# The first block of a two-layer kernel: the bias loaded and turned between the row tiles of x, the second half's turns elsewhere, nine of twelve products in 512 columns

## The chip, the cores and the metric

The kernel runs on one core of one Trainium2 chip. The metric is the device time of one execution in microseconds. Lower is better.

## The reference

```python
batch, m, k, h, n = 16, 512, 768, 3072, 768
y = np.matmul(x, w1) + b1          # x: 16 x 512 x 768, w1: 768 x 3072, b1: 3072
y = np.maximum(y, 0)
return np.matmul(y, w2)            # w2: 3072 x 768
```

All inputs and the output are float32. With the batch flattened x has 8192 rows.

## The kernel before

**Blocks.** The 8192 rows are cut into eight blocks of 1024 rows, and the 3072 hidden columns into two chunks of 1536. The kernel goes through the eight blocks with the first chunk, then through them again with the second: 16 rounds of a first phase (x times w1, bias, relu) and a second phase (the result y times w2). The weights of a chunk and one block of x lie in SBUF in float16. In most rounds both phases are done with fewer products than the plain scheme needs: sums and differences of tiles are formed first (VectorE; lines 828 for x, 844 for w1, 862 for w2, 1046 for y), the products of the sums are made on TensorE (line 1073 in the first phase, 1199 in the second), and their results are combined by VectorE and ScalarE (lines 1109 to 1124 and 1210 to 1216). A combination may also put a start value into the PSUM bank of a chain of products that follows, a "seed"; operation 16 of the first phase (line 1124) is one.

**The first block** (`first_block`, with the first chunk) is different. Its data have only just been loaded, so its first phase uses plain products. x arrives as row tiles of 128 rows and has to be turned (transposed) 128 x 128 at a time. The 1024 rows are eight row tiles: 0 to 3 are the first half (m = 0), 4 to 7 the second (m = 1). Tiles 0 to 3 come in float32 on the queues of SyncE and ScalarE (line 711), are turned by TensorE (line 925) into PSUM, and copied to `x` as float16, one part of each tile by VectorE (line 933) and one by ScalarE (line 931). Tiles 4 to 7 come through GpSimd's queue as float16 into `xn` (line 706) and are turned in the same way. w1 comes in six strips of 256 columns (line 685), w2 in twelve pieces (line 691), on GpSimd's queue too.

A product of the first block (`add_plain`, matmuls in line 983) is named by strip, by j (128 of the strip's 256 columns) and by the half m; it goes over 768 rows of w1 in six steps and has 512 columns of x. With `parts=2` it is made in two halves of 256 columns, 12 matmuls, of which the first half reads only the first two row tiles of its half of x; with `parts=1` in six matmuls of 512 columns, which need all four tiles. ScalarE applies bias and relu and writes y (line 992), for `evict_parts=2` in two pieces. Before the change the twelve products of the strips 0 to 2 all have `parts=2`; the twelve of the strips 3 to 5 have `parts=1`.

**The bias.** `load_bias` (line 679) loads it as 24 rows of 128 on ScalarE's queue. `add_bias` turns it on TensorE (line 945), copies it from PSUM (line 948, VectorE) and forms twelve small operations for the tables of the later rounds (lines 959 and 963) and one for a check (line 951), all on VectorE.

**What sets the order.** Every piece of work is a task of a planner (`Graph`): engine, expected length, what it reads and writes. TensorE's tasks run in the order in which they are added. For VectorE, ScalarE, GpSimd and SyncE the planner simulates the run and picks, among the tasks that can start, the one that is due first; some tasks are only fitted into gaps. It also picks the PSUM bank of each product or turn, among those that come free. `presets` gives it the times at which the first loads land, among them that of the bias (`b1_rows`). The instructions are then written in the planned order, and each engine runs its own in that order.

Of the kernel before, what the change touches and what calls it, by code (L numbers as in the profile page):

```python
# [586 lines left out]
class Fast:  # L587
# [120 lines left out]
    def prologue(self):  # L708
        nc = self.nc
        for s in range(4):  # L710
            (nc.sync, nc.scalar)[s % 2].dma_start(out=self.s[:, s],
                                                  in_=self.xf[s * P:(s + 1) * P, :])
        self.load_bias()
        self.load_strip(self.v1, 0, 0, 0)
        self.constants()
        self.load_strip(self.v1, 0, 0, 1)
        self.load_strip(self.v1, 0, 0, 2)
        self.load_x(0, 1, 2)
        for h in range(3):
            self.load_strip(self.v1, 0, 1, h)  # L720
        for q in range(4):
            for h in range(3):
                self.load_w2(self.v2, 0, h, q)
        self.load_x(1, 0)
        for _ in range(8):
            nc.tensor.matmul(self.ps[:, 7, 0:P], lhsT=self.ones, rhs=self.ones, start=True,
                             stop=True)

    def presets(self):
        g = self.g  # L730
        for t, at in enumerate((9.3, 11.3, 13.3, 19.9, 21.8, 23.8)):
            for k in range(2):
                g.preset(("w1", t // 3, 2 * (t % 3) + k), at)
        for q in range(4):
            for h in range(3):
                for n in range(2):
                    g.preset(("w2", 2 * q + n, h), 24.8 + 3 * q + h)
        for s in range(4):
            g.preset(("xn", 4 + s), 15.2 if s < 2 else 17.2)
            g.preset(("xn", s), 39.5)  # L740
            g.preset(("rows", s), (5.3, 5.3, 7.2, 7.2)[s])
        g.preset("b1_rows", 5.0)

# [264 lines left out]
    def first_block(self):  # L1010
        for s in range(4):
            self.add_transpose_first(0, s)
        plain = self.add_plain
        for strip in range(3):
            for j in range(2):
                between = None
                if strip == 0 and j == 0:
                    between = self.add_bias
                elif strip == 2 and j == 1:
                    between = lambda: [self.add_transpose_first(1, s) for s in (0, 1)]  # L1020
                plain(strip, j, 0, 2, 2 if strip == 1 else 1, between)
        plain(0, 0, 1, 2, 1, lambda: [self.add_transpose_first(1, s) for s in (2, 3)])
        plain(0, 1, 1, 2, 1)
        for strip in (1, 2):
            for j in range(2):
                plain(strip, j, 1, 2, 2 if strip == 1 else 1)
        for strip in (3, 4, 5):
            for m in range(2):
                for j in range(2):
                    plain(strip, j, m, 1, 1)  # L1030
# [514 lines left out]
```

## Time and profile before

| | |
|---|---|
| Device time, median of 3 runs | 849.0 us (848.92 to 849.01) |
| Span of the profiled execution | 847.4 us |
| TensorE busy | 839.4 us, 99% |
| VectorE busy | 737.9 us, 87% |
| ScalarE busy | 569.4 us, 67% |
| First product of the first block starts | 9.46 us |
| Second phase of the first block starts | 42.96 us |
| First phase of the second block starts | 68.31 us |

The profile is of one execution, and shows for every engine when each instruction ran and what ended the idle time ahead of it. Its span goes from the first instruction to the end of the last and is 1.6 us shorter than the median device time, which also counts what lies around it. PE is TensorE, PEld its weight load, DVE is VectorE, ACT ScalarE, POOL GpSimd and SP SyncE. In timelines a row is the start, the length, the engine, line and operation, what it writes and reads, how many neighbours of one kind are merged (x12), and in brackets the idle time ahead of it with what ended it. Times in the text are counted from the start of the span. Matmuls are pipelined and their recorded lengths overlap, so their rate is read from starts.

### The profile page before, as it was taken

The page shows a single profiled execution, that of the slowest core. Times are in us where ns is not written, and L with a number is a line of the kernel's source. Part 1 is how long each engine was busy: PE and PEld are TensorE (multiplying, and loading weights), DVE is VectorE, ACT ScalarE, POOL GpSimd, SP SyncE. Part 2 cuts the span into 40 slices and gives each one's busy share as a digit, 9 for nine tenths or more (in the row PEclk, how much of TensorE's full clock was granted, in tenths as well). Part 3 has the DMA queues.
Part 4 walks back from the last instruction along what each step waited for, and adds up shares of the span by engine and source line. Part 5 has one row for each costly group of instructions (what it writes and reads, how often), then busy time and mean ns, then how long its engine had stood idle before and what let it go on. Part 6 is the DMA issues. An engine that isn't in the chain of part 4 may idle for free. (4 is left out here: it accounts for less than half of the span.)

```text
span 847.4 us, 16784 instructions
## 1 busy us (share of the span) xinstructions
PE 839.4 (99%) x6381; PEld 625.5 (74%) x6381; DVE 737.9 (87%) x1231; ACT 569.4 (67%) x1203; POOL 164.1 (19%) x179
## 2 busy tenths in 40 slices
PE   8999999999999999999999999999999999999997
PEld 7558778686786867768687686877868678686874
DVE  5898987969889697998999979798896979979788
ACT  5866876778677695756858558766757666456463
POOL 5210011102111010010030503224041230501300
PEclk9999999999999999999999999999999999999999
DMA  9996497978988678594793977979789797985836
GB/s 213 202 180 176 81 233 105 163 183 133 222 113 148 169 126 192 95 223 150 224 187 65 192 123 124 187 106 178 125 128 150 116 173 113 147 134 75 146 117 169
DMA packets 170967, 128.93 MB, mean 152 GB/s; under 512 B 93804, under 2 KB 169348, under 8 KB 170884
## 3 DMA queue, kind: packets, MB, share of 16 engines
q0 software_dynamic: 56560, 68.82, 53.1%
q1 hardware_dynamic: 113856, 58.02, 28.3%
q8 instruction: 50, 0.82, 0.4%
q10 hardware_dynamic: 468, 1.00, 0.3%
q14 instruction: 33, 0.27, 0.1%
HBM read 73.54 MB, written 69.21 MB: 168 GB/s over the span
## 5 line engine op out<-in xcount | busy, mean ns | idle before, releaser
L1199 PE MATMUL ps<-v,y 128*128 128x384 f16 x2496 | 408.4, 326 | 0.0
L1073 PE MATMUL ps<-x,v 128*128 128x256 f16 x3600 | 395.7, 273 | 0.0
L1073 PEld LDWEIGHTS <-v 128*128 128x128 f16 x3600 | 352.2, 98 | 42.4 <-issue 0.2
L1199 PEld LDWEIGHTS <-y 128*128 128x128 f16 x2496 | 244.2, 98 | 160.0 <-issue 0.2
L1210 ACT ACTIVATE s<-ps 128x384 f32<-128x384 f32 (+1 forms) x244 | 153.0, 646 | 121.3 <-PE ps L1199 120.2
L1046 DVE TENSOR_TENSOR y<-y 128x768 f16<-128x768 f16 (+1 forms) x384 | 219.4, 619 | 2.6
L1116 DVE CUSTOM_DVE_ANT_0 y<-ps,s 128x512 f16<-128x512 f32 x240 | 156.0, 686 | 54.4 <-ACT s L1113 41.4
L1252 POOL DMA_DIRECT2D out_dram<-s x78 | 93.9, 1470 | 145.4 <-ACT s L1210 97.0
L1113 ACT ACTIVATE s<-ps,bt 128x256 f32<-128x256 f32 x180 | 75.3, 470 | 62.5 <-PE ps L1073 56.7
L828 DVE TENSOR_TENSOR x<-x 128x768 f16<-128x768 f16 (+1 forms) x210 | 113.7, 579 | 1.3
L1113 ACT ACTIVATE y<-ps,bt 128x256 f16<-128x256 f32 x180 | 69.5, 486 | 10.8 <-PE ps L1073 10.8
L1210 ACT ACTIVATE ps<-ps 128x384 f32<-128x384 f32 (+1 forms) x144 | 67.9, 509 | 8.1 <-PE ps L1199 6.6
L1216 DVE TENSOR_TENSOR s<-ps,s 128x768 f32<-128x768 f32 x74 | 70.5, 953 | 1.2 <-issue 0.3
L706 POOL DMA_DIRECT2D xn<-in_x_dram x30 | 25.9, 863 | 214.0 <-DMA x<-xn 99.5
L1216 DVE TENSOR_TENSOR s<-s,ps 128x768 f32<-128x768 f32 x60 | 57.1, 951 | 2.2 <-DVE s L1216 0.5
L767 ACT ACTIVATE junk<-xn 128x768 f16<-128x768 f16 x64 | 54.0, 843 | 0.3
L1255 POOL DMA_DIRECT2D out_dram<-s x15 | 17.7, 1181 | 169.5 <-ACT s L1210 157.7
L1113 ACT ACTIVATE ps<-ps,bt 128x256 f32<-128x256 f32 x60 | 26.7, 445 | 32.4 <-PE ps L1073 31.4
L1109 ACT ACTIVATE ps<-ps 128x512 f32<-128x512 f32 x60 | 35.3, 588 | 4.1 <-DVE y L1116 3.5
L1124 DVE TENSOR_TENSOR s<-s,ps 128x512 f32<-128x512 f32 x30 | 20.6, 688 | 17.7 <-PE ps L1073 17.7
L983 PE MATMUL ps<-x,v 128*128 128x256 f16 (+1 forms) x216 | 32.0, 308 | 0.7 <-DVE x L933 0.7
L1119 DVE SCALAR_TENSOR_TENSOR s<-ps,bt,s 128x256 f32<-128x256 f32 x60 | 26.1, 477 | 4.4 <-PE ps L1073 4.4
(60 smaller groups left out, 304.8 us busy)
## 6 DMA issues: line engine op xcount, KB each, us to landing
out_dram<-s POOLq DMA_DIRECT2D x93, 384.0 KB, 8.8
out_dram<-s SPq DMA_DIRECT2D x70, 384.0 KB, 6.6
xn<-in_x_dram POOLq DMA_DIRECT2D x28, 768.0 KB, 9.7
x<-out_dram SPq DMA_DIRECT2D x7, 384.0 KB, 3.5
v<-in_w_dram POOLq DMA_DIRECT2D x6, 384.0 KB, 10.6
v<-in_w_dram POOLq DMA_DIRECT2D x12, 192.0 KB, 9.1
w1d<-in_w_dram POOLq DMA_DIRECT2D x6, 384.0 KB, 6.5
w2d<-in_w_dram POOLq DMA_DIRECT2D x12, 192.0 KB, 4.9
```

The lines of the kernel that those rows point to most:

```text
L767: self.nc.scalar.activation(out=self.junk, in_=self.xn[:, s, :], func=ACTF.Square, accum_out=self.stat[:, self.stat_at["x"] + i:][:, 0:1])
L828: self.nc.vector.tensor_tensor(out=self.two(x, out), in0=self.two(x, in0), in1=self.two(x, in1), op=ALU.add if sign > 0 else ALU.subtract)
L983: nc.tensor.matmul(self.ps[:, ps.at[0], cols], lhsT=self.v1[:, gi, 2 * h + k2, k, j * P:(j + 1) * P], rhs=rhs, start=(k2 == 0 and k == 0), ...
L1046: self.nc.vector.tensor_tensor(out=self.two(self.y, out), in0=self.two(self.y, in0), in1=self.two(self.y, in1), op=ALU.add if sign > 0 els ...
L1073: nc.tensor.matmul(self.ps[:, at, j * self.QM:(j + 1) * self.QM], lhsT=self.v1[:, gi, self.w1s[c][gi][FIRST_V[p]], k, j * P:(j + 1) * P], ...
L1109: nc.scalar.activation(out=out, in_=ps, scale=float(a), func=func if kind == "out" else ACTF.Copy)
L1113: nc.scalar.activation(out=out[:, j], in_=ps[:, j], func=func, scale=float(a), bias=beta(j))
L1116: nc.vector._custom_dve(TENSOR_ADD_SAT, out=out, in0=ps, in1=s, s0=F_MAX, s1=0.0)
L1199: nc.tensor.matmul(self.ps[:, bank[ch].at[j], 0:NH], lhsT=self.y[:, ys[SECOND_U[p]], m0:m0 + P], rhs=self.v2[:, slot[SECOND_V[p]], h, :], ...
L1210: nc.scalar.activation(out=out, in_=ps, func=ACTF.Copy, scale=float(a))
L1216: engine.tensor_tensor(out=out, in0=in0, in1=in1, op=ALU.add if a == b else ALU.subtract)
L1252: nc.gpsimd.dma_start(out=rows, in_=out, accum_op=ALU.add)
```

## The change

It has four parts, all in the first block.

- The bias is loaded on ScalarE's queue between its two row tiles (1 and 3), and no longer behind both. The planner is told that it lands at 6.0 us instead of 5.0.
- The bias is turned after the row tiles 0 and 1 and ahead of 2 and 3, and no longer between the two halves of the first product.
- The turns of tiles 4 and 5 stand ahead of the product of strip 2, j = 1, and no longer between its halves. The turns of tiles 6 and 7 stay behind the first half of the first product of m = 1, but the whole product of j = 1 now comes behind them, ahead of that product's second half.
- Nine of the twelve products have `parts=1`. Two halves are kept for strip 0 with j = 0 and m = 0, and for strip 0 with m = 1 (both j). Every eviction is one piece.

```diff
@@ prologue
         for s in range(4):
             (nc.sync, nc.scalar)[s % 2].dma_start(out=self.s[:, s],
                                                   in_=self.xf[s * P:(s + 1) * P, :])
-        self.load_bias()
+            if s == 1:
+                self.load_bias()
@@ presets
-        g.preset("b1_rows", 5.0)
+        g.preset("b1_rows", 6.0)
@@ first_block
         for s in range(4):
             self.add_transpose_first(0, s)
+            if s == 1:
+                self.add_bias()
         plain = self.add_plain
+
+        def turns(*tiles):
+            for s in tiles:
+                self.add_transpose_first(1, s)
         for strip in range(3):
             for j in range(2):
-                between = None
-                if strip == 0 and j == 0:
-                    between = self.add_bias
-                elif strip == 2 and j == 1:
-                    between = lambda: [self.add_transpose_first(1, s) for s in (0, 1)]
-                plain(strip, j, 0, 2, 2 if strip == 1 else 1, between)
-        plain(0, 0, 1, 2, 1, lambda: [self.add_transpose_first(1, s) for s in (2, 3)])
-        plain(0, 1, 1, 2, 1)
+                if strip == 2 and j == 1:
+                    turns(0, 1)
+                plain(strip, j, 0, 2 if strip == 0 and j == 0 else 1, 1)
+        plain(0, 0, 1, 2, 1, lambda: [turns(2, 3), plain(0, 1, 1, 2, 1)])
         for strip in (1, 2):
             for j in range(2):
-                plain(strip, j, 1, 2, 2 if strip == 1 else 1)
+                plain(strip, j, 1, 1, 1)
```

## The prediction

> **What bounds the kernel now.** I read the page's head first, then the waits of TensorE, then TensorE's instructions in order of time, and last VectorE in the stretches where TensorE never waits.
>
> ```profile
> span 847.4 us, 16784 instructions
> PE 839.4 (99%) x6381; PEld 625.5 (74%) x6381; DVE 737.9 (87%) x1231; ACT 569.4 (67%) x1203; POOL 164.1 (19%) x179
> ```
>
> TensorE (PE) is busy for 839.4 of 847.4 us. The view of waits, for TensorE alone, says where the rest is:
>
> ```profile
> PE ps L726 <- DVE ones L666: 1.3, 1, 1.3
> PE ps L925 <- DMA s<-in_x_dram: 1.1, 2, 0.6
> PE ps L983 <- DVE x L933: 0.7, 2, 0.3
> ```
>
> Every wait belongs to the first block; L1073 and L1199, the lines of all later products, have none. So a microsecond won or lost in the first block reaches the end whole, as long as the other engines can follow. The timeline of TensorE (start, length, what, and the idle time ahead of it) shows the block:
>
> ```profile
> 5.55 1.50 PE L925 MATMUL ps<-ident,s 128*128 128x128 f32 x12 [0.48 <-DMA s<-in_x_dram]
> 7.64 1.50 PE L925 MATMUL ps<-ident,s 128*128 128x128 f32 x12 [0.58 <-DMA s<-in_x_dram]
> 9.46 0.82 PE L983 MATMUL ps<-x,v 128*128 128x256 f16 x6 [0.32 <-DVE x L933]
> 10.21 0.24 PE L945 MATMUL ps<-ident,b_rows 24*128 24x24 f32 x1
> 10.38 6.72 PE L983 MATMUL ps<-x,v 128*128 128x256 f16 x60
> 16.93 0.83 PE L925 MATMUL ps<-ident,xn 128*128 128x128 f16 x12
> 17.61 1.59 PE L983 MATMUL ps<-x,v 128*128 128x256 f16 x12
> 19.03 0.83 PE L925 MATMUL ps<-ident,xn 128*128 128x128 f16 x12
> 20.21 22.91 PE L983 MATMUL ps<-x,v 128*128 128x256 f16 x138 [0.35 <-DVE x L933]
> ...
> 42.96 25.51 PE L1199 MATMUL ps<-v,y 128*128 128x384 f16 x156
> 68.31 26.36 PE L1073 MATMUL ps<-x,v 128*128 128x256 f16 x240
> ```
>
> The lengths overlap by a pipeline's depth, so I go by starts. 60 matmuls of 256 columns run from 10.38 to 16.93: 0.1092 us each, 0.655 for six, which is half a product.
>
> **The change part by part.** The instruction order of the changed kernel, which can be built, differs on VectorE (DVE) only in its first 117 planned tasks, on ScalarE (ACT) in about its first 70, and on GpSimd and SyncE nowhere. From about 80 us on it is the same program. The question is therefore how many microseconds earlier TensorE comes out at 80 us.
>
> *Bias turn taken out of the first product.* Six matmuls start at 9.46 and the next six at 10.38: 0.92, where six take 0.655. The bias costs 0.265 there, and this goes. In its new place, after the first two tiles, TensorE ends at 5.55 + 1.50 = 7.05 and waits for row tile 2 until 7.64; the bias's 0.24 fits into that hole, if the bias has landed. For its landing:
>
> ```profile
> DMA to landing us min/median/max: 4.3/5.1/6.1
> ```
>
> This is the row tiles' line (L711): from issue to landing 4.3 us for the first, 6.1 for the last, so they land from 5.3 to 7.5. The bias now stands between ScalarE's two tiles. I take a landing before 7.05, at no cost, and keep 7.5 as the upper end. Row tile 3 is issued 0.65 us later, but needs to be there only when its turn comes, near 8.4 (the middle of the group of turns at 7.64), and the tile ahead of it in its queue lands only at 5.3. I cost it at nothing; landing after 8.4 it would cost one for one.
>
> *The bias tables now stand ahead of the tiles' copies.* This is the term that speaks against the change. VectorE's timeline of before:
>
> ```profile
> 6.11 1.21 DVE L933 CAST x<-ps 128x384 f16<-128x384 f32 x2 [4.87 <-PE ps L925]
> 8.19 1.21 DVE L933 CAST x<-ps 128x384 f16<-128x384 f32 x2 [0.87 <-PE ps L925]
> 10.48 0.18 DVE L948 COPY b1y<-ps 128x24 f32<-128x24 f32 x1 [1.07 <-PE ps L945]
> 10.70 0.24 DVE L959 TENSOR_SCALAR bt<-b1y 128x8 f32<-128x8 f32 x2
> 10.98 0.17 DVE L963 TENSOR_TENSOR bt<-bt,b1y 128x8 f32<-128x8 f32 x1
> 11.06 0.31 DVE L959 TENSOR_SCALAR bt<-b1y 128x8 f32<-128x8 f32 x3
> 11.41 0.17 DVE L963 TENSOR_TENSOR bt<-bt,b1y 128x8 f32<-128x8 f32 x1
> 11.49 0.17 DVE L959 TENSOR_SCALAR bt<-b1y 128x8 f32<-128x8 f32 x1
> 11.69 0.37 DVE L963 TENSOR_TENSOR bt<-bt,b1y 128x8 f32<-128x8 f32 x2
> ```
>
> In the changed order the copy of the bias and seven table operations stand between the copies of tile 1 and tile 2, and two more between tile 2 and tile 3. Eight such operations take 11.49 - 10.48 = 1.01; they start when tile 1's copy ends, at 7.32, so tile 2's copy starts at 8.33 instead of 8.19. It takes 0.6; two table operations, the second waiting for the first, take 0.20 + 0.08; so tile 3's copy starts near 9.2 and ends at 9.75, where it ended at 8.19 + 1.21 = 9.40. Neighbours that do not wait for each other overlap by up to 0.08, so the delay lies between about 0.15 and 0.35. Does TensorE wait for it? The first product reads only tiles 0 and 1, yet before it waited for "DVE x L933" until 9.46: it uses the PSUM bank that tile 3's copy leaves, and by the changed plan it still does. So the first product starts **0.25 later**. The first strip of w1 hides nothing of it; TensorE's weight load waited for it until 9.32 only:
>
> ```profile
> 9.32 0.67 PEld L983 LDWEIGHTS <-v 128*128 128x128 f16 x6 [0.42 <-DMA v<-in_w_dram]
> ```
>
> The Trainium skill, "VectorE: DVE Perf Modes", section "The DRAIN you can't avoid", says that the next operation does not start until the pipe is empty, and that a semaphore between two costs nothing extra. By that the ten operations would take their full lengths and the first product would start about 0.7 later. The row with three operations in 0.31 us speaks against it; it is a rival below.
>
> *The second half's turns.* The first pair (tiles 4 and 5) stood between two halves of a product and costs 17.61 - 16.93 = 0.68; so it does in its new place. The second pair takes 20.21 - 19.03 = 1.18, so **0.50** of it is a wait for the copies. Now half a product (0.655) that needs only tiles 4 and 5 comes behind it, more than the 0.50: the wait goes, with 0.15 to spare. The twelve matmuls at 17.61 take 19.03 - 17.61 = 1.42 instead of 1.31, a further **0.11** behind ScalarE's copy of tile 5, which ends at 17.47 + 0.86 = 18.33; a whole product of 1.3 us now covers it. That row, and those of the loads of x (L706):
>
> ```profile
> 17.47 0.86 ACT L931 COPY x<-ps 128x384 f16<-128x384 f16 x2 [0.30 <-PE ps L925]
> ```
>
> ```profile
> L706 POOL DMA_DIRECT2D xn<-in_x_dram x2: 718/726/735, 5.6 to 6.3; - x2
> ...
> DMA to landing us min/median/max: 9.5/10.1/10.8
> ```
>
> Tiles 4 and 5 land at 5.6 + 9.5 = 15.1, tiles 6 and 7 at 6.3 + 10.8 = 17.1. The new turns start near 9.71 + 1.31 + 4 x 1.30 = 16.2 and 18.8. Both in time.
>
> *Nine products in 512 columns.*
>
> ```profile
> L983 PE MATMUL ps<-x,v 128*128 128x512 f16 x72 | 15.7, 379 | 0.0
> ```
>
> From 20.21 to 42.96 run 66 matmuls of 256 and these 72 of 512: (22.75 - 66 x 0.1092) / 72 = 0.216 each. A product takes 1.296 instead of 1.310; nine save **0.13**. ScalarE's evictions in one piece save it time too, but it is no bound there.
>
> Shift of TensorE when the block ends: -0.265 - 0.50 - 0.11 - 0.13 + 0.25 = **-0.76 us**.
>
> *What is late next.* VectorE. It starts the sums of the last strips when the strip lands, at 23.72, and the strip does not land sooner because TensorE is early. From there it has hardly a gap:
>
> ```profile
> 23.72 1.15 DVE L844 TENSOR_TENSOR v<-v 128x768 f16<-128x768 f16 x2 [1.36 <-DMA v<-in_w_dram]
> ```
>
> ```profile
> 43.00:60.00 17.00, 16.93 (x28) 1.00 0.92 171
> 60.00:76.40 16.40, 15.98 (x27) 1.00 0.94 246
> 76.40:80.60 4.20, 2.16 (x5) 1.00 0.00 0
> ```
>
> (stretch, its length, VectorE's busy time.) Until 76.4 it is full; only then does it catch up. The changed order puts sums that nobody needs yet behind those that TensorE waits for, which covers TensorE's lead to about 75 us. But by operation 16 of the next block (L1124, the seed of chain 0) the same work is behind it in either order:
>
> ```profile
> 76.42 0.70 DVE L1124 TENSOR_TENSOR ps<-s,ps 128x512 f32<-128x512 f32 x1 [0.21 <-issue]
> ```
>
> It can start about 0.2 earlier, not 0.76: it ends between 76.7 and 76.9. The fifteenth product of the block reads it. It started at 68.31 + 14 x 0.655 = 77.48 and would now start at 76.72. I take **0.15 lost** there (bounds 0 and 0.3). After that VectorE idles, and the rest moves as one.
>
> Sum: -0.76 + 0.15 = -0.6 us: a span of 846.8. The span is 1.6 below the median of the runs; with the same around it, 849.0 becomes **848.4**.
>
> **The rivals.**
>
> 1. *Nothing lost on VectorE*: the table operations overlap fully, tile 3's copy is hidden and operation 16 is in time. -0.265 - 0.50 - 0.11 - 0.13 = -1.0: 848.0. For it: 0.21 us of VectorE's time before L1124 was idle. Against it: the first product waited for just this copy.
> 2. *VectorE takes it all back.* Between 43 and 76.4 it has 0.07 + 0.42 = 0.5 us of idle time to cover a lead of 0.76; if the new order makes one more gap, the lead is gone by 80 us: 848.9 to 849.0.
> 3. *Pipe drains between the small operations*: eight in 8 x 0.17 = 1.36 and two more in 0.34, tile 3's copy ends at 10.1, the first product starts 0.7 later; -1.0 + 0.7 = -0.3: 848.7. For it: those that wait for their neighbour are 0.20 apart. Against it: three in 0.31. It is the rule of the Trainium skill named above.
> 4. *The bias lands late, the other side.* TensorE runs in order, so the bias turn holds tiles 2 and 3, and VectorE's ten operations start 0.3 after it. Before, its landing was covered until 10.21. The moment that decides is about 7.7 us: then the first product starts 1.0 later than before and nothing is won; each microsecond beyond costs one. At 8.5 it is 849.8. Against it: the third issue of ScalarE, as the bias then was, already moved its data by 6.95:
>
> ```profile
> q10 hardware_dynamic: 50, 0.02, 9.4%
> ```
>
> (ScalarE's queue from 6.20 to 6.95 us: 50 packets of 0.4 KB on average, where a row of x has 3 KB and one of the bias 0.5 KB: this is the bias.) In front of tile 3 it can hardly be later.
>
> 5. *It does not do what it says*: the wait of 0.50 comes back at the second half of the product behind the turns, where tiles 6 and 7 are read. Then -0.6 + 0.5: 848.9.
>
> **How the numbers follow.** Forecast (848.1 to 848.7) 0.64; rival 1 0.10; rival 2 0.10; rival 3 0.06; rival 4 0.05; rival 5 0.05. The range: rival 1, with the 0.14 by which the first product could start before 9.46, gives 847.85; rival 2 with a stall of 0.15 more gives 849.15. So 847.8 to 849.2; outside it lies rival 4 and little else. 0.2% (1.7 us, about what a measurement of this kernel can tell from no change) is more than every term here together: to be faster by that, the block would have to lose more waiting than the 1.0 it has; to be slower, the bias would have to land after 9.4 us. Chances: faster 0.03, within 0.93, slower 0.04.
>
> **What would show it.** In the changed kernel's profile: the bias matmul near 7.0, inside the idle time ahead of 7.64; tile 3's copy on VectorE ending at 9.6 to 9.75, and the first product 0.05 behind it; two groups of turns near 16.2 and 18.8 without the 0.35 of idle time; L1199 first at 42.2; a short wait of TensorE at L1073 near 76.8 for "DVE ps L1124"; L1199 again at 93.9, 0.6 before the 68.31 + 240 x 0.1092 = 94.5 of now. A bias matmul after 7.7, a wait behind the second turns, or waits for VectorE between 43 and 75 us would prove me wrong.

## The result, and the profile after

The changed kernel takes **850.39 us** (median of 19 runs, 849.91 to 851.95); beside it on the same chip the kernel before takes 848.88 (19 runs, 848.82 to 849.15). The ratio is 1.0021, interval 1.0015 to 1.0028: 1.5 us slower, where 0.6 us faster was forecast (849.0 to 848.4), and above the forecast's range (847.8 to 849.2). The changed kernel's times also spread over 2 us, those of before over 0.3.

The profiled execution took 851.14 us, its span is 849.5, 2.1 more than before. I read it in the order of the forecast: TensorE's waits, its first instructions, then VectorE; and last the end of the kernel, which the forecast had not looked at. TensorE's waits in the changed kernel:

```profile
PE ps L984 <- DVE x L934: 1.8, 1, 1.8
PE ps L727 <- DVE ones L666: 1.3, 1, 1.3
PE ps L926 <- DMA s<-in_x_dram: 0.5, 1, 0.5
```

The three waits for DMA and VectorE of before have become one of 1.8 us. TensorE's timeline:

```profile
5.57 1.95 PE L926 MATMUL ps<-ident,s 128*128 128x128 f32 x12 [0.50 <-DMA s<-in_x_dram]
7.45 0.24 PE L946 MATMUL ps<-ident,b_rows 24*128 24x24 f32 x1
...
10.95 6.65 PE L984 MATMUL ps<-x,v 128*128 128x256 f16 x36 [1.79 <-DVE x L934]
17.44 0.83 PE L926 MATMUL ps<-ident,xn 128*128 128x128 f16 x12
18.11 2.11 PE L984 MATMUL ps<-x,v 128*128 128x512 f16 x12
20.06 0.83 PE L926 MATMUL ps<-ident,xn 128*128 128x128 f16 x12
20.73 22.85 PE L984 MATMUL ps<-x,v 128*128 128x256 f16 x114
43.41 25.51 PE L1202 MATMUL ps<-v,y 128*128 128x384 f16 x156
```

The first product starts at 10.95 instead of 9.46, 1.49 later. From there to the second phase it is 32.46 us instead of 33.50: 1.04 less, close to the 0.265 + 0.50 + 0.11 + 0.13 = 1.005 of the forecast. So the second phase starts 0.45 late.

Part of the 1.49 is TensorE's clock. The twelve turns at 5.57 take 1.95 instead of 1.50. In the trace the record of the granted clock begins, at 1.0, at 6.50 us in this run and at 5.54 in the profile of before; the turns start 0.21 to 0.24 apart ahead of that moment and 0.11 apart behind it. VectorE shows the rest:

```profile
7.23 0.56 DVE L934 CAST x<-ps 128x384 f16<-128x384 f32 x1 [0.19 <-PE ps L926]
7.72 0.18 DVE L949 COPY b1y<-ps 128x24 f32<-128x24 f32 x1
7.94 0.70 DVE L960 TENSOR_SCALAR bt<-b1y 128x8 f32<-128x8 f32 x2
8.68 0.17 DVE L964 TENSOR_TENSOR bt<-bt,b1y 128x8 f32<-128x8 f32 x1
8.76 0.71 DVE L960 TENSOR_SCALAR bt<-b1y 128x8 f32<-128x8 f32 x3
...
9.59 0.56 DVE L934 CAST x<-ps 128x384 f16<-128x384 f32 x1
```

Two table operations take 0.70 and three take 0.71, where before they took 0.24 and 0.31. One line's durations (least, median, most, in ns), of after:

```profile
L960 DVE TENSOR_SCALAR bt<-b1y x8: 163/169/629, 7.9 to 11.0; 128x8 f32<-128x8 f32 x8
```

and of before:

```profile
L959 DVE TENSOR_SCALAR bt<-b1y x8: 165/165/254, 10.7 to 12.1; 128x8 f32<-128x8 f32 x8
```

Most still take 0.17, but some take 0.63. What ran beside those? GpSimd, which writes the descriptors of the loads of w1:

```profile
6.96 2.50 POOL L685 DMA_DIRECT2D v<-in_w_dram  x3
9.98 0.70 POOL L691 DMA_DIRECT2D v<-in_w_dram  x1 [0.52 <-DMA v<-in_w_dram]
```

Three issues follow one another from 6.96 to 9.46. In the trace the second ends at 8.646 and the third at 9.463; the long operations of VectorE end at 8.643, 9.462 and 9.472. Not every one is held: the first, at 7.941, takes 0.172, although the second issue has run since 7.770. Before, GpSimd did the same from 6.98 to 9.47, but VectorE had its tables at 10.70.

Now the end. The branch behind the last product gives the point at which TensorE is through; after and before:

```profile
L1515 PEldq COMPARE_BRANCH  x2: 95/202/310, 841.9 to 843.2; - x2
...
L1515 PEldq EVENT_SEMAPHORE  x1: 51/51/51, 843.1 to 843.1; - x1
```

```profile
L1512 PEldq COMPARE_BRANCH  x2: 90/135/180, 841.3 to 842.6; - x2
...
L1512 PEldq EVENT_SEMAPHORE  x1: 51/51/51, 842.5 to 842.5; - x1
```

TensorE is through 0.6 later (843.1 against 842.5), but the span is 2.1 longer. **1.5 us are lost when TensorE has nothing left to do.** The view of the DMA from 840 to 850 us, in 40 slices of 0.25 us, of after:

```profile
GB/s 197 0 0 221 387 326 369 381 375 369 326 387 363 362 381 375 99 307 344 422 338 357 356 344 350 266 25 31 25 57 25 25 6 0 0 0 0 0 0 0
...
q8 instruction: 1, 0.02, 0.6%
...
out_dram<-s ACTq DMA_DIRECT2D x1, 192.0 KB, 4.3
out_dram<-s SPq DMA_DIRECT2D x1, 192.0 KB, 4.2
```

and of before:

```profile
GB/s 43 344 375 326 399 357 356 375 332 375 381 375 369 307 123 356 369 362 387 369 356 363 387 113 0 0 0 33 0 0 0 0 0 0 0 0 0 0 0 0
...
out_dram<-s ACTq DMA_DIRECT2D x1, 192.0 KB, 2.5
out_dram<-s SPq DMA_DIRECT2D x1, 192.0 KB, 2.6
```

Before, the stores run at about 370 GB/s and stop. After, they stop likewise, and then 25 GB/s go on for 1.5 us: about a sixteenth of the full rate, so one DMA engine of 16 works on alone. The last stores land after 4.2 instead of 2.6 us. What is new beside them is one packet of 16 KB in a queue of kind "instruction". In the trace it starts at 844.84 and takes 0.945 us; before, the last one of its kind runs at 837.4. Both kernels have 50 of these over the run. They follow TensorE's instructions (12,730 before, 12,620 after): from one packet to the next TensorE starts 255 matmuls and weight loads on average, so a packet holds about 256. In the trace the stores' packets keep 16.3 to 16.9 at a time busy where no such packet runs, and 15.2 to 15.9 from 844.4 to 845.8: about one engine of 16 is lost to them for 1.4 us. The packet is on record for 0.945 of that; what holds the engine ahead of it is not shown.

### The profile page after: what moved, and what is told of

The parts are those of the page before. It is cut to its first block, busy times and chain, and to the rows that moved or that the text cites. A ratio compares the mean times of both kernels' runs of the same rounds, so it can differ in the third digit from the quotient of the medians.

```text
span 849.5 us, 16673 instructions
## 1 busy us (share of the span) xinstructions
PE 839.4 (99%) x6327; PEld 620.6 (73%) x6327; DVE 738.6 (87%) x1231; ACT 568.5 (67%) x1199; POOL 164.0 (19%) x179
## 5 line engine op out<-in xcount | busy, mean ns | idle before, releaser
L1116 ACT ACTIVATE y<-ps,bt 128x256 f16<-128x256 f32 x180 | 69.5, 486 | 10.8 <-PE ps L1076 10.8
L984 PE MATMUL ps<-x,v 128*128 128x512 f16 (+1 forms) x162 | 31.6, 355 | 1.8 <-DVE x L934 1.8
## 6 DMA issues: line engine op xcount, KB each, us to landing
v<-in_w_dram POOLq DMA_DIRECT2D x6, 384.0 KB, 10.7
```

The source lines that it names most:

```text
L984: nc.tensor.matmul(self.ps[:, ps.at[0], cols], lhsT=self.v1[:, gi, 2 * h + k2, k, j * P:(j + 1) * P], rhs=rhs, start=(k2 == 0 and k == 0), ...
L1116: nc.scalar.activation(out=out[:, j], in_=ps[:, j], func=func, scale=float(a), bias=beta(j))
```

## The experiments

Two theories. **A**: the table operations with one input are held while GpSimd writes descriptors, and hold the copies of tiles 2 and 3 behind them; rival: so many small operations are simply long; second rival: TensorE's clock, which comes up at different times, makes tile 1 and all behind it late. **B**: with 110 instructions fewer on TensorE one more fetch of instructions falls among the last stores and delays them; rival: the late end follows from the late beginning. A third, **C**, came up on the way: a lead of TensorE is used up by 500 us in every plan. All numbers, with the difference to the kernel before on the same chip (us; "fetch" is a 16 KB instruction packet after 843):

| kernel | first product | second phase | last matmul starts | fetch | last store lands in | time | difference |
|---|---|---|---|---|---|---|---|
| before | 9.46 | 42.96 | 842.12 | no | 2.6 | 848.88 | |
| after | 10.95 | 43.41 | 842.73 | yes | 4.2 | 850.39 | +1.51 |
| two-input tables | 10.37 | 42.84 | 842.07 | yes | 4.4 | 850.15 | +1.19 |
| late tables | 9.59 | 42.36 | 842.12 | yes | 4.0 | 850.18 | +1.22 |
| before, 12 split | 9.24 | 42.91 | 842.23 | yes | 4.2 | 850.41 | +1.45 |
| after, 9 split | 10.19 | 42.78 | 842.10 | no | 2.6 | 848.99 | +0.03 |
| bias alone | 10.19 | 43.41 | 842.42 | no | 2.6 | 849.52 | +0.65 |
| turns alone | 9.30 | 42.34 | 841.36 | no | 2.6 | 848.19 | -0.68 |
| third part alone | 9.32 | 43.12 | 842.51 | yes | 4.1 | 850.99 | +2.12 |
| late tables, 9 split | 9.54 | 42.15 | 841.26 | no | 2.6 | 848.41 | -0.46 |
| bias alone, two-input | 9.72 | 42.98 | 842.50 | no | 2.6 | 849.74 | +0.82 |
| late tables, no nine | 9.68 | 42.46 | 842.31 | no | 2.6 | 849.00 | +0.08 |
| after, strip 1 in two | 10.19 | 42.76 | 842.66 | yes | 4.4 | 851.37 | +2.45 |

### The end: instructions added and taken away

The same edit in both kernels: some products of strips 3 to 5 run as two halves, inside the same planned operation.

```diff
         def product(n):
+            if parts == 1 and (gi):
+                for half in range(2):
...
+                            nc.tensor.matmul(
+                                self.ps[:, ps.at[0], half * self.QM:(half + 1) * self.QM],
...
+                return
```

In the kernel before all twelve are split, in the changed one nine. The planner believes that such a product leaves its PSUM bank as a whole one does (`leaves=2`). It doesn't, so the seeds that are put there next are not added in full; that part of the output differs, and no instruction is left out.

> The kernel before with one edit: the twelve products of strips 3 to 5 of the first block run as two halves of 256 columns each, inside the same planned operation, which adds 144 instructions to TensorE (12,874 instead of 12,730; the changed kernel has 12,620; the first and the last are nearly the same modulo 256, 74 and 76). Cost of the edit itself: 12 x 0.014 = 0.17 us. Theory B (TensorE's instructions are fetched in blocks of 16 KB, 256 instructions, by DMA; where the last fetch falls on the last stores, they land later): the last fetch moves from 837.4 to 844 to 846, the last stores take 4.0 us or more instead of 2.6, and the time is 1.0 to 1.7 us longer: 849.9 to 850.6. Rival (the late end of the changed kernel has another cause, such as its later start or chance): stores at 2.6, and 849.05, 0.17 more than before.

It took 850.41 (849.95 to 851.04), +1.45 us, ratio 1.0017 (1.0008 to 1.0026). The forecast for B was 849.9 to 850.6. From the same view as above, 840 to 850 us:

```profile
q8 instruction: 1, 0.02, 0.9%
...
out_dram<-s ACTq DMA_DIRECT2D x1, 192.0 KB, 4.3
out_dram<-s SPq DMA_DIRECT2D x1, 192.0 KB, 4.2
```

Its first block isn't late, TensorE's last matmul starts 0.11 later than before, and still the end is 1.3 us longer: the rival falls.

> The changed kernel with one edit: nine of the twelve products of strips 3 to 5 of the first block run as two halves of 256 columns, which gives TensorE 12,728 instructions, 2 fewer than the kernel before has. Cost of the edit itself: 9 x 0.014 = 0.13 us. Theory B: the last fetch falls at 837.5 to 839 again, the last stores take 2.6 us, and the time falls by 0.9 to 1.4 us, to 849.0 to 849.5, with the first product still at 10.9. Rival (the late end has another cause): 850.5, 0.13 more than the changed kernel.

It took 848.99 (848.93 to 849.72): 1.40 less than the changed kernel, though the first product is still 0.73 late and the edit itself costs 0.13. From 840 to 850 us no instruction packet of 16 KB is left, and

```profile
out_dram<-s SPq DMA_DIRECT2D x1, 192.0 KB, 2.6
```

**B holds, in both directions**: 1.4 to 1.5 us are the end, all of the changed kernel's loss.

The third part, as a last test of B, in the kernel before:

```diff
-                plain(strip, j, 0, 2, 2 if strip == 1 else 1, between)
+                plain(strip, j, 0, 2 if between else 1, 1, between)
...
-                plain(strip, j, 1, 2, 2 if strip == 1 else 1)
+                plain(strip, j, 1, 1, 1)
```

> The kernel before with the third part alone: nine of the twelve products in 512 columns, bias and turns where they were (12,633 instructions of TensorE, 97 fewer than before). All theories: the second phase about 0.1 early. Theory B: 97 instructions fewer put the last fetch at 842.5 to 844, among the last stores, which take 4 us or more to land instead of 2.6; 849.8 to 850.5. Rival (the late end of the changed kernel comes from its late first block): stores at 2.6, 848.75 to 848.95.

(This edit makes eight products whole, not nine: strip 2, j = 1 keeps its halves, because turns still stand between them. Eight times twelve instructions are 96 of the 97.)

It took 850.99 (850.57 to 851.99), +2.12: more than B's 849.8 to 850.5. The fetch is there at 844.1, the stores take 4.1. Beyond the end it lost something that no theory had: the second phase is 0.16 late instead of 0.1 early, and the last matmul 0.39 late. From the first product to the second phase it is 33.80 us, 0.30 more than before, because a product now waits for ScalarE's eviction, in TensorE's timeline:

```profile
30.17 13.11 PE L983 MATMUL ps<-x,v 128*128 128x512 f16 x60 [0.32 <-ACT y L992]
```

Its fetch corrects B in one point. I had put it at 842.5 to 844 by the count of instructions. But in all six kernels that have it, it comes 1.5 to 2.1 us after TensorE's last matmul starts, so it belongs to the branch to the end of the program, and the count of instructions decides whether it is needed. The numbers of instructions leave 74, 76 and 89 when divided by 256 where it comes, 184 to 186 where it doesn't. In the traces the branch itself takes 0.310 in all six with it and 0.180 in all seven without it (the pair of rows above has one of each). That its target lies in a block not yet fetched is argued from this, not shown. How long the packet takes differs, 0.945 to 1.61 us in the profiles, and the runs of the kernels that have it spread over 1.0 to 2.0 us, those of the others over 0.2 to 1.0.

### The beginning: the tables

```diff
-                nc.vector.tensor_scalar(out=out, in0=b, scalar1=float(coef), scalar2=None,
-                                        op0=ALU.mult)
+                zero = self.low[:, self.nstat - 8:].rearrange("p (c t) -> p c t", c=self.NCH)
+                nc.vector.tensor_tensor(out=out, in0=zero, in1=b,
+                                        op=ALU.add if coef > 0 else ALU.subtract)
```

> The changed kernel with one edit: the bias tables' six single-input operations (fp32 tensor_scalar on VectorE, line 960) become two-input ones (zero plus or minus the bias), in the same places and the same number. Theory A (a single-input fp32 operation of VectorE cannot start while GpSimd writes the descriptors of a DMA, and the tables stand ahead of the copies of x's tiles 2 and 3): none of the ten takes 0.6 us any more, all take 0.16 to 0.18; tile 2's copy starts at 8.5 to 8.9 instead of 9.59, the first product at 9.7 to 9.9 instead of 10.95, and the time falls by 1.0 to 1.2 us, to 849.2 to 849.4. Rival 1 (ten small dependent operations are long by themselves): the first product stays at 10.9 and the time at 850.4. Rival 2 (TensorE's clock, granted at half until 6.5 in the changed kernel's profile, made tile 1 and with it everything late): the first product comes at 10.3 to 10.9. The landing of the last stores stays at 4.2 us in all three.

(The rows count eight operations with one input and four with two; "six" and "ten" were miscounted.) All took 0.16 to 0.18, as A wants. But the first product came at 10.37, where A said 9.7 to 9.9 and rival 2, the clock, 10.3 to 10.9. In this run the record of the full clock begins at 6.95 only; the turns of tiles 0 and 1 took 2.17 us, so tile 1's copy started at 7.45. Both causes are at work. The time, 850.15, hardly moved, and the late end blurs it. So the same in a kernel without the late end. First the bias part alone, in the kernel before (the planner's 6.0 comes with it):

```diff
-        self.load_bias()
+            if s == 1:
+                self.load_bias()
...
+            if s == 1:
+                self.add_bias()
...
-                if strip == 0 and j == 0:
-                    between = self.add_bias
```

> The kernel before with the first part of the change alone: the bias loaded behind two of x's row tiles and turned between tiles 1 and 2; the turns of the second half and the products stay as before (12,728 instructions of TensorE, 2 fewer than before). Theory A (tables held by GpSimd's descriptor writing, and the copies of tiles 2 and 3 behind them): the first product at 10.2 to 11.0 instead of 9.46, 0.27 of that given back by the bias turn that no longer stands in it, and the wait of the second turns shorter by what remains; the second phase 0.2 to 0.8 late; no fetch near the end, stores at 2.6; 849.1 to 849.7. Rival (the tables cost the forecast 0.25): first product at 9.7, 848.8 to 848.95.

It took 849.52 (849.30 to 850.29), +0.65, and the first product is 0.73 late, in TensorE's timeline:

```profile
10.19 7.37 PE L984 MATMUL ps<-x,v 128*128 128x256 f16 x66 [1.41 <-DVE x L934]
```

A's numbers; its rival expected 9.7 and at most 848.95. Then with the two-input tables of the diff above, in a run whose turns took 1.50 as in that one (full clock from 5.05 here and from 5.35 there):

> The run with the bias part alone, with the six single-input operations of the tables made two-input ones, as in the first experiment; its end has no late fetch, so that the first block can be read in the time. Theory A: all ten at 0.16 to 0.18, the first product at 9.6 to 9.9 instead of 10.19, and 0.2 to 0.5 us less than the bias part alone: 849.0 to 849.3. Rival (their number alone delays the copies): first product at 10.2, 849.5.

The durations of the table's line (least, median, most) with one input and with two, and the first product with two in TensorE's timeline:

```profile
L960 DVE TENSOR_SCALAR bt<-b1y x8: 162/318/617, 7.5 to 10.2; 128x8 f32<-128x8 f32 x8
```

```profile
L961 DVE TENSOR_TENSOR bt<-low,b1y x8: 157/160/168, 7.6 to 9.7; 128x8 f32<-128x8 f32 x8
```

```profile
9.72 7.37 PE L985 MATMUL ps<-x,v 128*128 128x256 f16 x66 [1.00 <-DVE x L934]
```

The same operations in number, place and size, beside the same issues of GpSimd, and the first product comes 0.47 earlier. **A holds for the place where it acts.** Its price in time did not follow: 849.74 (849.27 to 850.02) instead of 849.0 to 849.3. Beside the kernel before on its chip that is +0.82, where the kernel with one input has +0.65, and the runs of the two overlap. TensorE's lead over that kernel, 0.47 at the first product and 0.43 at the second phase, was down to 0.06 behind this wait:

```profile
61.88 6.99 PE L1201 MATMUL ps<-v,y 128*128 128x384 f16 x42 [0.21 <-DVE s L1218]
```

The tables can also be moved. They are queued behind tile 3's copy:

```diff
-                      reads=["b1y"], writes=[("bt", n)])
+                      reads=["b1y"], writes=[("bt", n)], after=after)   # after tile 3's copy
```

> The changed kernel with the bias turned in the same place, but the ten table operations and the squares of the check queued behind the copy of tile 3 instead of ahead of the copies of tiles 2 and 3. Theory A (GpSimd's descriptor writing holds the tables, and they hold the copies) and its rival of plain length both expect the first product at 9.4 to 9.7 and 1.2 to 1.5 us off the time: 848.9 to 849.2; the single-input operations may still show 0.2 to 0.7 us where a descriptor issue runs beside them, and nobody waits for that. Rival 2 (the clock makes tile 1 late): 10.0 or later and 849.6 or more. If the time went under 848.7, the late end of the stores would not be there, which would speak against theory B.

The first product came at 9.59, as expected, so nothing but the tables and the late clock had delayed it (here the full clock is on record from 4.53; TensorE's timeline, what it waits for now is w1):

```profile
9.59 6.67 PE L990 MATMUL ps<-x,v 128*128 128x256 f16 x36 [0.90 <-DMA v<-in_w_dram]
```

But 850.18 instead of 848.9 to 849.2: TensorE's lead of 0.60 at the second phase was gone at the end.

### Does a lead reach the end?

That lead shrank from 0.59 to 0.39 at 69 us, to 0.16 at 418 and to nothing at 494. In two other kernels with the plan of after it was also gone at 494. So theory C. First the second part alone, in the kernel before:

```diff
-                    between = lambda: [self.add_transpose_first(1, s) for s in (0, 1)]
+                    turns(0, 1)
...
-        plain(0, 0, 1, 2, 1, lambda: [self.add_transpose_first(1, s) for s in (2, 3)])
-        plain(0, 1, 1, 2, 1)
+        plain(0, 0, 1, 2, 1, lambda: [turns(2, 3), plain(0, 1, 1, 2, 1)])
```

> The kernel before with the second part alone: the turns of the second half at their new places (12,729 instructions of TensorE, 1 fewer than before). All theories: the first product as before, the second phase about 0.6 early (42.3 to 42.4). Theory C (from 400 us on TensorE is held by others at the same times in every plan; a lead is used up there, only a lag is carried to the end): the lead is 0.2 or less by 500 us, and 848.7 to 848.95. Rival, as forecast (0.15 given back, the rest carried): 848.3 to 848.5. Stores at 2.6 in both.

It took **848.19** (848.08 to 848.29), ratio 0.9992 (0.9983 to 1.0001; so by this interval alone it is not clear of no change), the fastest of all here: all of its 11 runs lie below all 30 runs of the kernel before beside it (848.74 and more). The second phase in TensorE's timeline:

```profile
42.34 25.51 PE L1202 MATMUL ps<-v,y 128*128 128x384 f16 x156
```

The lead of 0.61 was 0.76 at the end. **C falls**; the forecast's reading is right here. The first product was 0.16 early in this run, at 9.30, and not as before.

Then the changed kernel with late tables and, against the late end, nine products of strips 3 to 5 planned in halves:

```diff
-                    plain(strip, j, m, 1, 1)
+                    plain(strip, j, m, 1 if strip == 5 and (m or j) else 2, 1)
```

> The changed kernel with both causes out: the tables behind the copy of tile 3, and nine of the twelve products of strips 3 to 5 planned as two halves of 256 columns (12,728 instructions of TensorE). First product at 9.4 to 9.7, second phase 0.4 to 0.6 early, last fetch near 837, stores at 2.6. Theory C: the lead is gone by 500 us, 848.7 to 849.0, no better than the kernel before. Rival, as forecast (a lead of the first block reaches the end): 848.3 to 848.5.

848.41 (848.05 to 849.04), ratio 0.9995 (0.9986 to 1.0004), so the time alone decides nothing; but the profile shows a lead of 0.81 at the second phase, 0.86 at the last matmul. C falls again. Last, late tables and the products as in the kernel before:

```diff
-                plain(strip, j, 0, 2 if strip == 0 and j == 0 else 1, 1)
+                plain(strip, j, 0, 2, 2 if strip == 1 else 1)
...
-                plain(strip, j, 1, 1, 1)
+                plain(strip, j, 1, 2, 2 if strip == 1 else 1)
```

> The changed kernel without its third part (all products in the columns of the kernel before, 12,728 instructions of TensorE) and with the tables behind the copy of tile 3: first product at 9.3 to 9.7, the second phase 0.7 to 0.85 early, last fetch near 836, stores at 2.6; 848.0 to 848.3. If the tables cost something at their later place, or the lead is lost on the way, 848.4 or more.

It differs from the last one in which products are whole and in strip 1's evictions, which are in two pieces again, and took 849.00 (848.54 to 849.20). Its lead of 0.50 went as C had said, the larger part by 70 us, behind this wait:

```profile
69.52 25.05 PE L1083 MATMUL ps<-x,v 128*128 128x256 f16 x228 [0.23 <-DVE s L1226]
```

and the rest, with 0.2 more, at 434 to 440 us. So a lead of half a microsecond survives in some plans and not in others.

One of those losses could be followed. In five kernels one operation of ScalarE near 493 us starts 0.33 after its last release instead of 0.05, and the idle time ahead of it in the timeline is 0.56 instead of 0.28. After, and before:

```profile
493.04 0.84 ACT L1116 ACTIVATE s<-ps,bt 128x256 f32<-128x256 f32 x2 [0.56 <-PE ps L1076]
```

```profile
492.32 0.84 ACT L1113 ACTIVATE s<-ps,bt 128x256 f32<-128x256 f32 x2 [0.28 <-PE ps L1073]
```

These five have 1,459 instructions on ScalarE. The next kernel puts back the four that the change saved there:

```diff
-                plain(strip, j, 1, 1, 1)
+                plain(strip, j, 1, 1, 2 if strip == 1 else 1)      # and likewise for m = 0
```

> The changed kernel with the four evictions of strip 1 in two parts each, as the kernel before has them: 1,463 instructions of ScalarE instead of 1,459. In the five kernels with 1,459 so far one ScalarE operation at 492.4 to 493.0 started 0.33 after its last release, in those with 1,458, 1,463 and 1,464 about 0.05 after it, and TensorE lost 0.18 there. Theory D (it goes with the place of that instruction in ScalarE's stream, so a fetch): the gap is 0.05 again, TensorE's lag does not grow at 494, and the time is 0.1 to 0.2 less than the changed kernel's, 850.2 to 850.3, with the stores at 4.2 still. Rival (it comes of the places of the buffers in the changed plan): the gap stays at 0.3 and the lag grows by 0.18.

The gap is closed:

```profile
492.88 0.84 ACT L1116 ACTIVATE s<-ps,bt 128x256 f32<-128x256 f32 x2 [0.28 <-PE ps L1076]
```

As built, this kernel and the changed one give every matmul and every VectorE operation the same buffers, and every ScalarE operation behind 25 us too. So the rival falls, and this loss goes with the place in ScalarE's stream. That a fetch is behind it is not shown.

The time did not follow: 851.37 (850.36 to 852.35), not 850.2. A new wait at 419 us took more than the gap had. The ScalarE operation that it names was late because the one ahead of it, a conversion of w2 (line 853), had waited for its load until 417.46; in the profile of before the same conversion started at 416.50 without a wait. The wait:

```profile
419.06 10.88 PE L1202 MATMUL ps<-v,y 128*128 128x384 f16 x66 [0.39 <-ACT ps L1213]
```

## Why the prediction was wrong

*The step that failed first is one that it did not have.* Its sum ends where TensorE ends, and it carries the rest of the span over from before as a constant ("the same around it"). That rest grew by 1.5 us, because the nine products take 108 instructions out of TensorE's stream and the waits 2 more. No term and no rival held this. Shown by adding and taking away instructions.

*"So the first product starts 0.25 later"* is the term that was mis-sized: 1.49 in the profile. The lengths of the operations were right: with two-input tables and turns of 1.50 us the first product came at 9.72, and the forecast's sum gives 9.71. What was missing is that the rows of before were taken at 10.7 to 11.5 us, when GpSimd was idle, and used for 7.9 to 9.5, when it was not. That costs 0.47 in the pair of bias kernels. In the changed kernel tile 2's copy starts 1.26 after the 8.33 of the forecast: 0.47 of it because tile 1's copy ended at 7.79 instead of 7.32, and the other 0.79 falls into the stretch of the tables. That is a count, not two separate prices, because a held operation ends with an issue of GpSimd: in "after, strip 1 in two" tile 1's copy ended at 7.71, only 0.08 sooner, and the first product came at 10.19, 0.76 sooner. The row at 11.98 was a warning: among eight operations one took 0.254, and in the trace it is the one beside the next issue of GpSimd, at 11.55.

The Trainium skill has the rule, in "SBUF — State Buffer", "Who interferes with whom": VectorE and GpSimd share a pair of SBUF ports, whoever starts first has it for the whole instruction, and the other is blocked; `tensor_scalar` can ask for the pair in a two-port mode, `tensor_tensor` takes only its read side, and writing descriptors needs the write side (these last two points the page infers). The trace agrees on who is held: up to 0.63 against 0.17 for one, 0.16 to 0.17 for the other in the same stretch, and the blocked ones end with the issue. It differs on the whole instruction: the operation at 7.941 passed in 0.172 inside a recorded issue. The forecast weighed another rule on these operations (the pipe's drain) and missed this one.

*The turns of tiles 0 and 1* were taken at 1.50, as one profile had them. They took 1.50 to 2.17 in the profiles of the twelve kernels that show them as a group, and the clock decides it: 1.50 in the five whose record of the full clock begins at 5.54 us or earlier, and longer where it begins later, from 1.65 (5.84) to 2.17 (6.95). (The views print a granted clock of 1.00 also ahead of the first record.) Before, waits for a tile of x and for w1 cover this: in "before, 12 split" the record begins at 6.95 too, and the first product comes at 9.24. With the tables ahead of tiles 2 and 3 nothing covers it. The matmuls ahead of the turns start at 1.29 in all profiles; why the clock comes up at 4.33 in one and at 6.95 in another stays open.

*The bias turn (-0.265), the second turns (-0.50 and -0.11), the nine products (-0.13)*: together 1.005 forecast, 1.04 measured, in the changed kernel. With the turns alone, the stretch from the first product to the end of the second turns was 0.61 shorter (10.14 us instead of 10.75), just their two terms; that the second phase came 0.61 early too is chance, since the 0.16 by which that run began earlier was lost again at 38 to 40 us. Eight whole products alone did not give their 0.11: from the first product to the second phase that kernel took 0.30 longer.

*"From about 80 us on it is the same program"*: the order is the same, but, in the programs as built, not the places in PSUM (they differ until about 403 us) and in the buffer `s` (to the end), nor the position of every instruction in its stream. Hence the 0.18 lost at 494.

*"A microsecond won or lost in the first block reaches the end whole"*: true in "turns alone" and "late tables, 9 split", not in "late tables" or "late tables, no nine". A view of waits says where TensorE waited with the present timing, not how little is missing elsewhere. Why one plan keeps the lead and another loses it was not settled. The 0.15 lost at operation 16 did not arise in the changed kernel, since TensorE was late there and not early. It did not arise with a lead either: in "turns alone" operation 16 starts at 75.99, 0.43 sooner, not 0.2, and the lead of 0.61 passes it whole. Where a lead was lost in this stretch, it was lost earlier, at 69.5 us in "late tables, no nine", to another operation of VectorE.

*The rivals*: 1 (nothing lost on VectorE) falls with the first product. 2 (VectorE takes the lead back by 80 us) had no lead to act on here, but "late tables, no nine" shows it: 0.40 of 0.50 gone by 70 us. 3, the pipe drains, falls: with two-input tables three operations still took 0.31, and the first product came at 9.72, not 0.7 late. 4: the bias was turned at 7.45, directly behind the first tiles, so it was not late; but the forecast's other side was this rival alone, with 0.05. 5 did not happen. Taken without its late end, the changed kernel is 848.99 - 0.13 (the split) = 848.9, an estimate: the time of rival 2, by another way.

## What to carry to other kernels

A duration from a profile holds for what ran beside it: before moving a short VectorE operation, look at what GpSimd does at the new time, and keep single-input fp32 operations that others wait for away from its DMA issues. Forecast the end of the span as well as the end of the bounding engine: where the last stores end it, anything that shares their DMA engines counts, instruction fetches too. Parts of a change that seem to belong together should be run alone: here the turns alone gain 0.7 us, the bias part alone loses 0.65, and the third part alone loses 2.1.

## What was unexpected of the hardware

- TensorE's instructions come in packets of 16 KB, about 256 instructions, over the same DMA engines as the data, 50 in a run, 0.9 to 1.8 us each in the kernel before. One among the last stores costs 1.4 to 1.5 us.
- A VectorE operation of 0.17 us took up to 0.63 beside GpSimd's descriptor writing; the same with two inputs took 0.16.
- The twelve turns at 5.5 to 5.7 us took 1.50 to 2.17 us from kernel to kernel, as the full clock came at 4.33 to 6.95 us.
- One instruction of ScalarE started 0.28 us later or not, depending on four instructions more or fewer ahead of it, and TensorE lost 0.18 by it.
